# Earlier operands at a seam, additions by twos, a second attention output tile and a second load queue in a fused block kernel

## The chip, the cores and the metric

The kernel runs on one core of one Trainium2 chip. The metric is the device time of one execution in microseconds (us); of several executions the median is given. Five engines work side by side, each on its own list of instructions: PE (matrix multiplies), DVE and ACT (element by element), POOL and SP (here almost only the issuing of transfers). An instruction whose input or output tile is not yet free blocks everything behind it in the list of its engine.

## The reference, cut to what matters

```
h = rmsnorm(x, norm_g)                              # 2048 tokens x 1024
q, k, v, z_att, gb, gc, u, z_conv, g_att, g_conv = split(h @ w_in)   # 1024 x 6144
att    = chunked_rel_attention(q, k, v, rel_bias)   # 8 heads of 64, a band of 9 chunks of 64 tokens
y_att  = (att * silu(z_att)) @ w_att_out            # 512 x 1024
y_conv = (gb * causal_conv3(gc * u) * silu(z_conv)) @ w_conv_out
m = sigmoid(g_att) * y_att + sigmoid(g_conv) * y_conv
x = x + m @ w_out                                   # 1024 x 1024
out = rmsnorm(x, final_norm_g)
```

Everything is float32.

## The kernel before

**Split numbers.** Every float32 operand is held as two tiles: a rounded high part, cast by ACT (`nc.scalar.copy`), and the rest, subtracted by DVE (`nc.vector.tensor_sub`). `split_into` does that for weights (L130, L131), `split_pair` for tokens (L136, L137). A product is then three matmuls per 128 rows of depth: high by high (L143), high by low (L144), low by high (L145), in `passes`.

**Products of blocks.** The big projection takes the tokens in two halves of 1024, each as two chunks of 512 (`CH`), and the 6144 columns as 24 pairs of two 128-column tiles (`NPAIR`). For one pair and one half, tokens, weights and results form 2 by 2 blocks, and the four result blocks come from seven block products, i = 1 to 7, in place of eight, with sums and differences of blocks as operands. One block product is four depth tiles by three passes, twelve matmuls of 128 x 512. The token operands `t{i}{j}` (product i, depth tile j) are made once for each half by `operand_steps`: for i = 6, 4 and 5 one DVE addition or subtraction (L363, L365, L369), and then the split on ACT and DVE. The weight operands `wc` of a pair are made by `operand(p, i)`, three block products ahead, and kept in DRAM for the second half (L408, L390, both on SP).

**The plain stage.** The first three pairs (`PLAIN`) of the first half are multiplied plainly, before the tokens are normalized, as twelve items q = 0 to 11 of 24 matmuls each (result `ps_p`, copied by ACT to `plain`, L727). This stage is in a `tc.manual_schedule`: there PE, DVE and ACT do the work in the order of the code. `between(q)` puts `steps` of `operand_steps` behind items 6 to 10, one operand i each; behind item 10 (`c and n == 0` of the last pair) two calls of `operand` make the weights of the products 1 and 2 of the first block pair. Everywhere else a scheduler sets each engine's order, and `seq` is the order of the block products.

**Attention.** From the second half on, attention runs interleaved with the block products: scores into `ps_s` (L199) with the bias and the minimum on DVE (L205), exponential and scaling on ACT (`pr`, L209, L211), transposes into `ps_t` (L219), the split of these into `pt` (ACT L224, DVE L225), and the product with the values into `po` (L234). `po` is added up into the output tile `o` of a pair of heads (DVE, L239, L240); when a chunk of 512 tokens of the pair is done, `o` is multiplied by `z`, split into `zs` and `o`, and both are stored by POOL as `mid` (L248). The tile `o` exists once. POOL also loads the attention's operands, among them `q` (L165) and `zs` (L187).

**Output projections.** `half_c` multiplies the `mid` tiles by `wy`, `half_d` the sum by `w_out`. The first sixteen `mid` tiles (those of the convolution) are loaded by SP (`load_mid`, L566) near the end of the block products.

Of the kernel before, what the change touches and what calls it, by code (L numbers as in the profile page):

```python
# [8 lines left out]
F32 = mybir.dt.float32  # L9
# [8 lines left out]
P = 128  # L18
# [5 lines left out]
CH = 512  # L24
NC = SEQ // CH
HEADS = 8
DH = 64
# [6 lines left out]
PLAIN = 3  # L34
# [8 lines left out]
def block_kernel(ctx, tc, xb, xt, wp_in, wy, wo, bias, ng, fg, cw, cb, out):  # L43
    nc = tc.nc
    pool = lambda name, bufs=1, **k: ctx.enter_context(tc.tile_pool(name=name, bufs=bufs, **k))

    const = pool("const")
    small = pool("small", 3)
    dram = pool("dram", 1, space=DRAM)

    ident = const.tile([P, P], F32, name="ident")
# [22 lines left out]
    def inverse_rms(v, n):  # L74

        y = small.tile([P, n], F32, name="ry", tag="ry")
        a = small.tile([P, n], F32, name="ra", tag="ra")
        q = small.tile([P, n], F32, name="rq", tag="rq")
        nc.vector.tensor_scalar(y.bitcast(I32), v.bitcast(I32), -0.5, 0x5F3759DF, op0=ALU.mult, op1=ALU.add)
        nc.vector.tensor_mul(a, y, v)  # L80
        nc.vector.scalar_tensor_tensor(a, a, THIRD, y, op0=ALU.mult, op1=ALU.mult)
        nc.vector.scalar_tensor_tensor(q, a, -10.0 / 3.0 * THIRD, a, op0=ALU.add, op1=ALU.mult)
        nc.vector.scalar_tensor_tensor(y, q, 5.0 * THIRD * THIRD, y, op0=ALU.add, op1=ALU.mult)
        nc.vector.tensor_mul(a, y, v)
        nc.vector.scalar_tensor_tensor(a, a, -0.5 / D_MODEL, y, op0=ALU.mult, op1=ALU.mult)
        nc.vector.scalar_tensor_tensor(y, a, 1.5, y, op0=ALU.add, op1=ALU.mult)
        return y

    def rms_of(acc, n):

        v = small.tile([P, n], F32, name="rv", tag="rv")
        nc.vector.scalar_tensor_tensor(v, acc[:, 0:2 * n:2], D_MODEL * EPS, acc[:, 1:2 * n:2], op0=ALU.add, op1=ALU.add)
        return inverse_rms(v, n)

# [23 lines left out]
    def defer(n, fn):  # L118
        later.append([n, fn])
# [20 lines left out]
    def passes(ps, w, rhs, cs=slice(0, CH), first=True, last=True, onto=False):  # L140

        for k, (rh, rl) in enumerate(rhs):
            nc.tensor.matmul(ps, lhsT=w[:, 0, k, :], rhs=rh[:, cs], start=(first and not onto and k == 0), stop=False, skip_group_check=onto)  # L143
            nc.tensor.matmul(ps, lhsT=w[:, 0, k, :], rhs=rl[:, cs], start=False, stop=False, skip_group_check=onto)  # L144
            nc.tensor.matmul(ps, lhsT=w[:, 1, k, :], rhs=rh[:, cs], start=False, stop=(last and k == len(rhs) - 1), skip_group_check=onto)  # L145


    def attention(ab):
# [35 lines left out]
        def load_z(c, h):  # L184
            if h % 2 == 0:
                zs = at([P, CH], "zs", F32)
                dma(zs, z_d[h // 2][c])  # L187
                pair[c, h // 2] = (zs, at([P, CH], "o", F32))

        def att_s(c, h, g):  # L190
            q, kk, bs = heads[c, h]
# [154 lines left out]
    def split_t(half, i, j, src):  # L346
        ops[half, i, j] = split_pair(f"t{i}{j}", src)
# [9 lines left out]
    def operand_steps(half):  # L357

        b11, b12, b21, b22 = (blocks[half, c, k] for k in range(2) for c in range(2))
        for i in ORDER:  # L360
            for j in range(4):
                if i == 6:
                    nc.vector.tensor_add(b11[:, j, :], b11[:, j, :], b12[:, j, :])  # L363
                elif i == 4:
                    nc.vector.tensor_sub(b21[:, j, :], b21[:, j, :], b11[:, j, :])  # L365
                src = {1: b11, 2: b21, 6: b11, 7: b12, 4: b21, 3: b22}.get(i)
                if i == 5:
                    t1 = e("t1")
                    nc.vector.tensor_sub(t1, b22[:, j, :], b11[:, j, :])  # L369
                split_t(half, i, j, t1 if i == 5 else src[:, j, :])  # L370
            yield i


# [73 lines left out]
    def ev_v(pr):  # L447
        def ev(g, c, src):
            t = copied_out(src)

            def turn():
                ps = bank("vt") if g < 2 else dbank("vt")
                for b in range(4):
                    nc.tensor.transpose(out=ps[:, b * P:(b + 1) * P], in_=t[:, b * P:(b + 1) * P], identity=ident)
                defer(0, lambda: split(ps))

            def split(ps):
                for b in range(2):
                    st = e("vst").rearrange("p (n d) -> p n d", d=P)
                    s = ps[:, b * 256:(b + 1) * 256].rearrange("p (n d) -> p n d", d=DH)  # L460
                    nc.scalar.copy(st[:, :, :DH].bitcast(F32R), s)
                    nc.vector.tensor_sub(st[:, :, DH:].bitcast(F32R), s, st[:, :, :DH])
                    v4 = st.rearrange("p (b h) d -> p b h d", h=2)
                    for h in range(2):
                        n = g % 2 * 4 + 2 * b
                        defer(1, lambda h=h, v4=v4, n=n: store(v_d[2 * pr + h][g // 2][:, n:n + 2, :], v4[:, :, h, :]))

            defer(1, turn)
        return ev
# [90 lines left out]
        nc.sync.dma_start(r4, src)  # L560
        return r4

    def load_mid(i, b, c):
        t = [slot("mid") for s in range(2)]
        for s in range(2):
            nc.sync.dma_start(t[s].bitcast(F32), mid_d[i][b][s][c])  # L566
        return t

    def gate(i, d, c, make):
# [92 lines left out]
    nw = 0  # L662
# [19 lines left out]
        return ss  # L682

    def rsqrt_of(ss):
        v = small.tile([P, 4], F32, name="rv", tag="rv")
        nc.vector.tensor_scalar_add(v, ss[:, 0:8:2], D_MODEL * EPS)
        return inverse_rms(v, 4)

    def between(q):

        if q == 4 or q == 5:
            for k in range(8):
                normalize(tt_[q - 4][k], k, rb[q - 4])
        elif q == 6:
            for j in range(4):
                third(0, j)
        if q > 5 and len(built) < 5:
            built.append(next(steps))

    engines = {mybir.EngineType.PE, mybir.EngineType.DVE, mybir.EngineType.Activation}  # L700
# [1 line left out]
    with tc.manual_schedule(engines=engines):  # L702
        for k in range(2):
            weights0(0, 0, k)
            for j in range(4):
                raw_split(0, 4 * k + j, tt_[0][4 * k + j])
        for k in range(2):
            weights0(0, 1, k)
        for k in range(8):
            square(0, k)  # L710
        for q, (p, n, c) in enumerate(plain):
            if q == 2:
                ss[0] = sums_of(0)
            elif q == 4:
                rb[0] = inverse(ry[0], e)
                store(rb_d[0], rb[0])
            ps = dbank("ps_p")
            for k in range(2):
                if k and q == 4:
                    ss[1] = sums_of(1)  # L720
                    ry[1] = rsqrt_of(ss[1])
                elif k and q == 5:
                    rb[1] = inverse(ry[1], e)
                    store(rb_d[1], rb[1])
                passes(ps, wops0[p, n, k], [raw_ops[c, 4 * k + j] for j in range(4)], slice(0, CH), k == 0, k == 1)
            t = e("plain")
            nc.scalar.copy(t, ps)  # L727
            store(plain_d[q], t)
            between(q)
            if q == 0:  # L730
                for j in range(8):
                    raw_split(1, j, tt_[1][j])
            elif q == 1:
                for k in range(4):
                    square(1, k)
            elif q == 2:
                ry[0] = rsqrt_of(ss[0])
                for k in range(4, 8):
                    square(1, k)
            if c and p + 1 < PLAIN:  # L740
                for k in range(2):
                    weights0(p + 1, n, k)
            elif c and n == 0:
                for _ in range(2):
                    operand(*seq[nw])
                    nw += 1
    x1 = None
    nbias = 0
    att = None
# [7 lines left out]
    for s, (p, i) in enumerate(seq):  # L757
# [17 lines left out]
        if n == 5 and i == 1:  # L775
            for c in range(2):
                for k in range(2):
                    load_x(1, c, k)
            x1 = norm_steps(1)
        ev = evs[p % NPAIR]  # L780
        g0, g1 = 2 * half, 2 * half + 1
        onto = half == 0 and i in (6, 5, 4, 3)
# [82 lines left out]
        if n == 2 * NPAIR - 1 and i == 5:  # L865
            made = make_c(0, ITEMS_C[0], e)
            rbs = [fslot("rbs") for c in range(2)]
            for c in range(2):
                nc.sync.dma_start(rbs[c], rb_d[c])
            mids = {c: [load_mid(1, b, c) for b in range(4)] for c in (0, 1)}  # L870
    while later:
        tick()
    for _ in ab:
# [34 lines left out]
    pair_slot = lambda: op.tile([P, 2, CH], F32R, tag="op", name="wo")  # L908
    wide_slot = lambda: wtile("wo").rearrange("p s k c -> p s (k c)")

    def half_c(hf, mids, made):

        cs = (2 * hf, 2 * hf + 1)
        c0, c1 = cs
# [25 lines left out]
        for n_, (i, d) in enumerate(ITEMS_C):  # L940
            raw, gl = made
            if n_ + 1 < len(ITEMS_C):
                made = make_c(hf, ITEMS_C[n_ + 1])
            w = wtile("wy")
            split_into(w, raw)
            if d < PLAIN and not hf:
                for c in cs:
                    nc.vector.tensor_mul(gl[c], gl[c], rbs[c])
# [199 lines left out]
        elif n == 3:  # L1148
            nxt["made"] = make_c(1, ITEMS_C[0])

    half_d(0, half_c(0, mids, made), next_half)
    half_d(1, half_c(1, nxt["mids"], nxt["made"]), lambda n: None)


# [49 lines left out]
```

## Time and profile before

| | |
|---|---|
| median of 3 runs | 1495.09 us (1494.68 to 1496.42) |
| the profiled execution, device time | 1495.93 us |
| its span in the trace | 1494.2 us |
| TensorE clock granted, mean | 0.997 of full |
| PE busy | 1474.8 us (99%) |
| DVE, ACT, POOL busy | 1074.0, 743.7, 163.8 us |
| plain stage, block products, output projections | to about 78, about 78 to 1157, from about 1157 us |

Times of places in the program count from the start of the span. A line such as L143 is line 143 of the kernel before. A row of the timeline gives start, duration, engine, line, operation, output<-input, shape and count, and in brackets how long the engine had been idle and what released it. A row of the waits gives who waits, at which line, for whom, the total in us, how often, and the longest. SPq stands for issues by SP.

### The profile page before, as it was taken

Reading aid. Unit: us, or ns where it says so; the run is one execution under the profiler, and the core shown is the slowest. Engines: PE = TensorE matmul, PEld = TensorE weight load, DVE = VectorE, ACT = ScalarE, POOL = GpSimd, SP = SyncE. Lnnn points to the kernel's source line nnn. Section 1 sums busy time; section 2 is a strip of 40 time slices with the busy share of each in tenths; the row PEclk is TensorE's granted clock in tenths of the full one; section 3 lists DMA queues with packets and bytes.
Section 4 is the critical chain, followed back from the end, with each engine's and each line's share of the span. In section 5 each row is a group of like instructions: output and inputs, shape, how many; then the busy total and the mean of one; then the engine's idle time right before and its main releaser. Section 6 shows DMA issues by size and latency. Waiting matters only on the chain. (4 is left out here: it accounts for less than half of the span.)

```text
span 1494.2 us, 21053 instructions
## 1 busy us (share of the span) xinstructions
PE 1474.8 (99%) x6976; PEld 1225.2 (82%) x6976; DVE 1074.0 (72%) x2100; ACT 743.7 (50%) x1407; POOL 163.8 (11%) x310
## 2 busy tenths in 40 slices
PE   9999999999999999999999999999999999999997
PEld 6878888888888788888888888788888788888886
DVE  7877567686568684766777778787766588767787
ACT  7454444444346333555666666566665333423153
POOL 0000000000000002323222233322220000010000
PEclk9999999999999999999999999999999999999999
DMA  6389999989989976999999787787889845877443
GB/s 235 104 308 334 336 323 331 372 315 330 323 299 329 342 288 234 322 359 346 308 293 286 243 269 256 237 261 257 271 278 324 296 152 173 304 261 232 155 162 113
DMA packets 169325, 409.33 MB, mean 274 GB/s; under 512 B 21120, under 2 KB 41600, under 8 KB 169216
## 3 DMA queue, kind: packets, MB, share of 16 engines
q1 hardware_dynamic: 139312, 320.67, 62.1%
q0 software_dynamic: 22272, 73.42, 15.4%
q10 hardware_dynamic: 7632, 13.90, 2.5%
q8 instruction: 55, 0.90, 0.2%
q14 instruction: 54, 0.44, 0.1%
HBM read 252.19 MB, written 155.71 MB: 273 GB/s over the span
## 5 line engine op out<-in xcount | busy, mean ns | idle before, releaser
L209 ACT ACTIVATE pr<-ps_s,nmax 128x640 f32<-128x640 f32 (+4 forms) x128 | 93.4, 730 | 94.6 <-DVE nmax L205 93.9
L165 POOL DMA_DIRECT2D q<-q x128 | 66.8, 526 | 662.9 <-DVE wc L131 572.8
L211 ACT ACTIVATE pr<-pr,rs 128x640 f32<-128x640 f32 (+4 forms) x128 | 97.8, 764 | 36.0 <-DVE rs L210 35.6
L205 DVE CUSTOM_DVE_ANT_0 ps_s<-ps_s,bs 128x640 f32<-128x640 f32 (+4 forms) x128 | 95.2, 744 | 23.3 <-PE ps_s L199 22.1
L131 DVE TENSOR_TENSOR wc<-wraw,wc 128x512 fp32r<-128x512 f32 x120 | 81.7, 685 | 30.9 <-ACT wc L130 30.6
L143 PE MATMUL ps_d<-mid,wy 128*128 128x512 f32 x256 | 100.1, 391 | 1.4 <-ACT wy L130 0.8
L144 PE MATMUL ps_d<-mid,wy 128*128 128x512 f32 x256 | 99.7, 390 | 0.2 <-DMA mid<-mid 0.2
L199 PE MATMUL ps_s<-kk,q 128*128 128x320 f32 (+1 forms) x448 | 98.3, 334 | 1.5 <-ACT pr L209 0.9
L145 PE MATMUL ps_d<-mid,wy 128*128 128x512 f32 x256 | 99.6, 390 | 0.0
L130 ACT CAST wc<-wraw 128x512 fp32r<-128x512 f32 x120 | 73.7, 621 | 46.0 <-PE ps_c L145 20.0
L225 DVE TENSOR_TENSOR pt<-ps_t,pt 128x640 fp32r<-128x640 f32 (+4 forms) x128 | 94.0, 735 | 3.4 <-ACT pt L224 2.5
L224 ACT CAST pt<-ps_t 128x640 fp32r<-128x640 f32 (+4 forms) x128 | 79.9, 624 | 21.2 <-PE ps_t L219 20.0
L219 PE MATMUL ps_t<-ident,pr 128*128 128x128 f32 x560 | 82.3, 273 | 1.3 <-DVE pt L225 1.2
L234 PE MATMUL po<-pt,vv 128*128 128x512 f32 x336 | 75.2, 355 | 0.3 <-DVE pt L225 0.3
L219 PEld LDWEIGHTS ps_t<-ident,pr 128*128 128x128 f32 x560 | 65.6, 140 | 11.4 <-DVE pt L225 1.6
L234 PEld LDWEIGHTS po<-pt,vv 128*128 128x128 f32 x336 | 62.4, 188 | 14.2 <-DVE pt L225 1.2
L199 PEld LDWEIGHTS ps_s<-kk,q 128*128 128x128 f32 x448 | 67.3, 189 | 6.6 <-ACT pr L209 5.8
L1001 PE MATMUL ps_w<-wo,lefth 128*128 128x512 f32 (+1 forms) x240 | 71.9, 382 | 0.0
L903 ACT ACTIVATE wo<-wor 128x512 fp32r<-128x512 f32 x56 | 34.5, 630 | 60.6 <-DMA wor<-wo 42.2
L143 PEld LDWEIGHTS ps_d<-mid,wy 128*128 128x128 f32 x256 | 48.1, 188 | 12.8 <-ACT wy L130 1.2
L145 PEld LDWEIGHTS ps_d<-mid,wy 128*128 128x128 f32 x256 | 48.1, 188 | 10.5 <-DVE wy L131 0.5
L144 PEld LDWEIGHTS ps_d<-mid,wy 128*128 128x128 f32 x256 | 48.1, 188 | 10.3 <-DMA mid<-mid 0.5
(557 smaller groups left out, 4089.5 us busy)
## 6 DMA issues: line engine op xcount, KB each, us to landing
wc<-wc SPq DMA_DIRECT2D x294, 512.0 KB, 5.4
wraw<-wp_in SPq DMA_DIRECT2D x54, 512.0 KB, 5.7
q<-q POOLq DMA_DIRECT2D x128, 128.0 KB, 4.9
mid<-mid SPq DMA_DIRECT2D x64, 256.0 KB, 5.5
wor<-wo SPq DMA_DIRECT2D x56, 256.0 KB, 5.0
gl<-gate SPq DMA_DIRECT2D x52, 256.0 KB, 2.9
bs<-bias POOLq DMA_DIRECT2D x32, 320.0 KB, 7.6
v<-vst SPq DMA_DIRECT2D x64, 128.0 KB, 4.4
```

The source lines that it names most:

```text
L131: nc.vector.tensor_sub(w[:, 1], src, w[:, 0].bitcast(F32))
L143: nc.tensor.matmul(ps, lhsT=w[:, 0, k, :], rhs=rh[:, cs], start=(first and not onto and k == 0), stop=False, skip_group_check=onto)
L144: nc.tensor.matmul(ps, lhsT=w[:, 0, k, :], rhs=rl[:, cs], start=False, stop=False, skip_group_check=onto)
L145: nc.tensor.matmul(ps, lhsT=w[:, 1, k, :], rhs=rh[:, cs], start=False, stop=(last and k == len(rhs) - 1), skip_group_check=onto)
L199: nc.tensor.matmul(ps[:, i, :m], lhsT=q[s][:, g * P:(g + 1) * P], rhs=kk[:, k1 - n + i * m:k1 - n + (i + 1) * m], start=(s == 0), stop=(s ...
L205: nc.vector.tensor_tensor_reduce(out=view, in0=view, in1=bv, scale=-0.125, scalar=3.0e38, op0=ALU.add, op1=ALU.min, accum_out=nmax)
L209: nc.scalar.activation(out, view, AF.Exp, bias=nmax, scale=-1.0, accum_out=rs)
L211: nc.scalar.activation(pr[:, :n], pr[:, :n], AF.Identity, scale=rs)
L219: nc.tensor.transpose(out=ps[:, j * P:(j + 1) * P], in_=pr[:, j * P:(j + 1) * P], identity=ident)
L224: nc.scalar.copy(hi[:, js, qs], src)
L225: nc.vector.tensor_sub(lo[:, js, qs], src, hi[:, js, qs].bitcast(F32))
L234: nc.tensor.matmul(ps[:, :, a * P:b * P], lhsT=vv[:, g0 + j, :], rhs=pt[:, j, :, a * P:b * P], start=(i == 0), stop=(i == len(js) - 1))
```

## The change

1. **End of the plain stage.** One weight operand is made before the copy of item 10 in place of two behind it, the second one follows that copy; the plain stage takes four token operands (1, 2, 6, 7) and not five; and the first half makes its token operands in the order 1, 2, 6, 7, 5, 4, 3, in which its products use them.
2. **Tokens two at a time.** In `operand_steps` two additions (or subtractions) stand ahead of their two splits, in place of addition, split, addition, split. This holds for both halves.
3. **V stores.** V is split for each head apart, and 32 stores of 4 x 128 per partition take the place of 64 of 2 x 128.
4. **Output tile.** `o` gets two buffers; two of the small vector pools go from three buffers to two for the space.
5. **First `mid` tiles.** POOL loads them in place of SP.
6. **First weights of the output projection.** `wy0` is allocated and split in the code of the last block product, and handed to `half_c`.

```diff
     small = pool("small", 3)
+    two = pool("two", 2)
...
-                pair[c, h // 2] = (zs, at([P, CH], "o", F32))
+                pair[c, h // 2] = (zs, at([P, CH], "o", F32, 2))
...
-        for i in ORDER:
-            for j in range(4):
-                if i == 6:
-                    nc.vector.tensor_add(b11[:, j, :], b11[:, j, :], b12[:, j, :])
-                elif i == 4:
-                    nc.vector.tensor_sub(b21[:, j, :], b21[:, j, :], b11[:, j, :])
-                src = {1: b11, 2: b21, 6: b11, 7: b12, 4: b21, 3: b22}.get(i)
-                if i == 5:
-                    t1 = e("t1")
-                    nc.vector.tensor_sub(t1, b22[:, j, :], b11[:, j, :])
-                split_t(half, i, j, t1 if i == 5 else src[:, j, :])
+        for i in ORDER if half else (1, 2, 6, 7, 5, 4, 3):
+            src = {1: b11, 2: b21, 6: b11, 7: b12, 4: b21, 3: b22}.get(i)
+            at = [None if i == 5 else src[:, j, :] for j in range(4)]
+            for js in ((0, 1), (2, 3)):
+                for j in js:
+                    if i == 6:
+                        nc.vector.tensor_add(at[j], at[j], b12[:, j, :])
+                    elif i == 4:
+                        nc.vector.tensor_sub(at[j], at[j], b11[:, j, :])
+                    elif i == 5:
+                        at[j] = e("t1")
+                        nc.vector.tensor_sub(at[j], b22[:, j, :], b11[:, j, :])
+                for j in js:
+                    split_t(half, i, j, at[j])
             yield i
...
-                for b in range(2):
+                p4 = ps.rearrange("p (n h d) -> p n h d", h=2, d=DH)
+                for h in range(2):
...
-                    for h in range(2):
-                        n = g % 2 * 4 + 2 * b
-                        defer(1, lambda h=h, v4=v4, n=n: store(v_d[2 * pr + h][g // 2][:, n:n + 2, :], v4[:, :, h, :]))
+                    n = g % 2 * 4
+                    defer(1, lambda h=h, st=st: store(v_d[2 * pr + h][g // 2][:, n:n + 4, :], st))
...
-        if q > 5 and len(built) < 5:
+        if q > 5 and len(built) < 4:
             built.append(next(steps))
...
+            if q == 4 * PLAIN - 2:
+                operand(*seq[nw])
+                nw += 1
             t = e("plain")
             nc.scalar.copy(t, ps)
...
-                for _ in range(2):
-                    operand(*seq[nw])
-                    nw += 1
+                operand(*seq[nw])
+                nw += 1
...
+        if s == len(seq) - 1:
+            wy0 = wtile("wy")
+            split_into(wy0, made[0])
...
-            mids = {c: [load_mid(1, b, c) for b in range(4)] for c in (0, 1)}
+            mids = {c: [load_mid(1, b, c, nc.gpsimd.dma_start) for b in range(4)] for c in (0, 1)}
...
-    half_d(0, half_c(0, mids, made), next_half)
+    half_d(0, half_c(0, mids, made, wy0), next_half)
```

How the order of instructions moves is shown at three places; line numbers of after stand one to ten higher.

On ACT, at the end of the plain stage, before the change (`t73h` is the last split of operand 7, `t40h` to `t43h` are those of operand 4; `plain` is the result of item 10 and then of 11; `wc` are the weights of products 1 and 2):

```order
L136 CAST t73h_1161<-xs_558 128x512
L727 COPY plain_1190<-ps_p_1165 128x512
L136 CAST t40h_1194<-xs_553 128x512
L136 CAST t41h_1199<-xs_553 128x512
L136 CAST t42h_1204<-xs_553 128x512
L136 CAST t43h_1209<-xs_553 128x512
L130 CAST wc_1213<-wraw_572 128x512
L130 CAST wc_1216<-wraw_572 128x512
L727 COPY plain_1244<-ps_p_1219 128x512
```

And after the change:

```order
L137 CAST t73h_1164<-xs_561 128x512
L131 CAST wc_1193<-wraw_575 128x512
L733 COPY plain_1196<-ps_p_1168 128x512
L131 CAST wc_1199<-wraw_575 128x512
L131 CAST wc_1231<-s2_1233 128x512
L131 CAST wc_1239<-wraw_577 128x512
L733 COPY plain_1227<-ps_p_1202 128x512
L131 CAST wc_1262<-s1_1232 128x512
```

The first `wc` stands directly behind `t73h`; the splits of operand 4 have gone from this stretch, and the weights of products 6 and 7 (`s2` and the next `wraw`) stand in it.

On DVE, in one of the attention's steps late in the second half, before the change (`c` and `u` are results of block products, `ot` and `o` the attention's output, `pt` the split of the transposed weights, ISA the bias and minimum of the scores):

```order
L798 TENSOR_TENSOR c_9641<-u,ps_d 128x512
L239 TENSOR_TENSOR ot<-po,ot 64x256
L240 TENSOR_TENSOR o<-po,ot 64x256
L225 TENSOR_TENSOR pt<-ps_t,pt 128x5x128
L205 ISA ps_s,nmax<-ps_s,bs 128x2x320
L205 ISA nmax 128x1
L820 TENSOR_TENSOR u<-u,ps_d 128x512
L210 RECIPROCAL rs<-rs 128x1
```

And after the change:

```order
L806 TENSOR_TENSOR c_9612<-u,ps_d 128x512
L240 TENSOR_TENSOR ot<-po,ot 64x256
L241 TENSOR_TENSOR o<-po,ot 64x256
L206 ISA ps_s,nmax<-ps_s,bs 128x2x320
L206 ISA nmax 128x1
L226 TENSOR_TENSOR pt<-ps_t,pt 128x5x128
L211 RECIPROCAL rs<-rs 128x1
L828 TENSOR_TENSOR u<-u,ps_d 128x512
```

`o` stands at the same place in the list, the scores' reduction has moved ahead of `pt`, and `rs` ahead of `u`; with two buffers the `o` of this step is another tile than the one still being stored.

On SP near the end of the block products, before the change (`mid1` are the stored tiles of the convolution, the last four of sixteen; `mid0` are the attention's):

```order
L566 DMA mid_11863<-mid1_2_0_1_268 128x512
L566 DMA mid_11864<-mid1_2_1_1_272 128x512
L566 DMA mid_11867<-mid1_3_0_1_276 128x512
L566 DMA mid_11868<-mid1_3_1_1_280 128x512
L566 DMA mid_11910<-mid0_0_0_0_219 128x512
```

After the change the same loads stand on POOL, behind the load of the last `z` and ahead of the stores of the last attention output:

```order
L569 DMA mid_11834<-mid1_2_0_1_271 128x512
L569 DMA mid_11835<-mid1_2_1_1_275 128x512
L569 DMA mid_11838<-mid1_3_0_1_279 128x512
L569 DMA mid_11839<-mid1_3_1_1_283 128x512
L249 DMA mid0_3_0_3_249<-zs_11492 128x512
L249 DMA mid0_3_1_3_253<-o_11494 128x512
```

On SP the loads of `mid0` then follow the last `wc` directly. The rows of ACT around the first cast of `wy` (behind the last `zs`) read alike in both orders: part 6 moves no row there.

More of the change, by code (lines that the diff above doesn't have):

```diff
@@ L76, in inverse_rms @@
         y = small.tile([P, n], F32, name="ry", tag="ry")
-        a = small.tile([P, n], F32, name="ra", tag="ra")
+        a = two.tile([P, n], F32, name="ra", tag="ra")
         q = small.tile([P, n], F32, name="rq", tag="rq")
@@ L89, in rms_of @@
     def rms_of(acc, n):
-        v = small.tile([P, n], F32, name="rv", tag="rv")
+        v = two.tile([P, n], F32, name="rv", tag="rv")
         nc.vector.scalar_tensor_tensor(v, acc[:, 0:2 * n:2], D_MODEL * EPS, acc[:, 1:2 * n:2], op0=ALU.add, op1=ALU.add)
@@ L457, in split @@
             def split(ps):
-                for b in range(2):
+                p4 = ps.rearrange("p (n h d) -> p n h d", h=2, d=DH)
+                for h in range(2):
                     st = e("vst").rearrange("p (n d) -> p n d", d=P)
-                    s = ps[:, b * 256:(b + 1) * 256].rearrange("p (n d) -> p n d", d=DH)
+                    s = p4[:, :, h, :]
                     nc.scalar.copy(st[:, :, :DH].bitcast(F32R), s)
                     nc.vector.tensor_sub(st[:, :, DH:].bitcast(F32R), s, st[:, :, :DH])
-                    v4 = st.rearrange("p (b h) d -> p b h d", h=2)
-                    for h in range(2):
-                        n = g % 2 * 4 + 2 * b
-                        defer(1, lambda h=h, v4=v4, n=n: store(v_d[2 * pr + h][g // 2][:, n:n + 2, :], v4[:, :, h, :]))
+                    n = g % 2 * 4
+                    defer(1, lambda h=h, st=st: store(v_d[2 * pr + h][g // 2][:, n:n + 4, :], st))
             defer(1, turn)
@@ L561, in raw_w, with load_mid @@
         return r4
-    def load_mid(i, b, c):
+    def load_mid(i, b, c, dma=nc.sync.dma_start):
         t = [slot("mid") for s in range(2)]
         for s in range(2):
-            nc.sync.dma_start(t[s].bitcast(F32), mid_d[i][b][s][c])
+            dma(t[s].bitcast(F32), mid_d[i][b][s][c])
         return t
@@ L684, in rsqrt_of @@
     def rsqrt_of(ss):
-        v = small.tile([P, 4], F32, name="rv", tag="rv")
+        v = two.tile([P, 4], F32, name="rv", tag="rv")
         nc.vector.tensor_scalar_add(v, ss[:, 0:8:2], D_MODEL * EPS)
@@ L909, in block_kernel, with half_c @@
     wide_slot = lambda: wtile("wo").rearrange("p s k c -> p s (k c)")
-    def half_c(hf, mids, made):
+    def half_c(hf, mids, made, ready=None):
         cs = (2 * hf, 2 * hf + 1)
@@ L943, in half_c @@
                 made = make_c(hf, ITEMS_C[n_ + 1])
-            w = wtile("wy")
-            split_into(w, raw)
+            w, ready = ready, None
+            if w is None:
+                w = wtile("wy")
+                split_into(w, raw)
             if d < PLAIN and not hf:
```

## The prediction

> **What bounds the kernel now.** I read the page's shares first, then what PE waited for, then the timeline around each wait.
>
> ```profile
> PE 1474.8 (99%) x6976; PEld 1225.2 (82%) x6976; DVE 1074.0 (72%) x2100; ACT 743.7 (50%) x1407; POOL 163.8 (11%) x310
> DMA  6389999989989976999999787787889845877443
> ```
>
> PE is busy for all but 1494.2 − 1474.8 = 19.4 us. The change removes no matmul, so it can win only PE's gaps and what follows from them: a matmul issued at half pace counts as busy. The second line is the share of the transfer engines in tenths, per fortieth of the span: often 9, so a queue may be a limit that PE's busy time hides.
>
> The waits of PE (at which line, for whom, total us, how often, longest):
>
> ```profile
> PE ps_c L143 <- ACT wc L130: 2.6, 1, 2.6
> PE ps_t L219 <- DVE pt L225: 1.2, 2, 1.0
> PE ps_d L143 <- DMA wc<-wc: 1.1, 1, 1.1
> PE ps_s L199 <- ACT pr L209: 0.9, 1, 0.9
> PE ps_d L143 <- ACT wy L130: 0.8, 1, 0.8
> PE po L234 <- DVE pt L225: 0.3, 1, 0.3
> PE ps_c L145 <- DVE wc L131: 0.3, 1, 0.3
> ```
>
> Each is a single place, not a steady shortage. The windows (from:to and length; busy us and count of PE, PEld, DVE, ACT, POOL; granted clock; DMA share; GB/s) show what else the two largest places cost:
>
> ```profile
> 75.00:112.00 37.00, 34.42 (x145) 27.95 (x144) 27.81 (x45) 19.96 (x36) 0.00 (x0) 0.95 0.87 310
> 112.00:150.00 38.00, 38.00 (x170) 31.45 (x169) 27.07 (x46) 15.99 (x27) 0.00 (x0) 1.00 0.93 333
> 934.00:972.00 38.00, 36.04 (x186) 30.40 (x185) 27.11 (x59) 22.72 (x41) 11.31 (x21) 0.96 0.74 237
> ```
>
> The granted clock is 0.95 and 0.96 there, and 1.00 in the undisturbed middle row. So a gap there costs its own length and a stretch at lower clock behind it.
>
> **Part 1, the end of the plain stage.** The timeline (start, duration, instruction; in brackets the idle time before it and its releaser):
>
> ```profile
> 71.98 0.62 ACT L136 CAST t73h<-xs 128x512 fp32r<-128x512 f32 x1
> 72.89 0.68 DVE L137 TENSOR_TENSOR t73l<-xs,t73h 128x512 fp32r<-128x512 f32 x1
> 78.17 0.62 ACT L136 CAST t42h<-xs 128x512 fp32r<-128x512 f32 x1 [1.36 <-DVE xs L365]
> 78.37 0.39 PE L145 MATMUL ps_p<-rawh,w 128*128 128x512 f32 x1
> 80.15 0.62 ACT L136 CAST t43h<-xs 128x512 fp32r<-128x512 f32 x1 [1.36 <-DVE xs L365]
> 80.67 1.14 ACT L130 CAST wc<-wraw 128x512 fp32r<-128x512 f32 x2
> 81.34 0.50 PE L143 MATMUL ps_c<-t10h,wc 128*128 128x512 f32 x1 [2.58 <-ACT wc L130]
> 85.36 0.39 PE L145 MATMUL ps_c<-t12h,wc 128*128 128x512 f32 x1
> 91.83 0.69 DVE L137 TENSOR_TENSOR t53l<-t,t53h 128x512 fp32r<-128x512 f32 x1
> 93.97 0.39 PE L143 MATMUL ps_c<-t50h,wc 128*128 128x512 f32 x1
> 96.69 0.39 PE L143 MATMUL ps_c<-t10h,wc 128*128 128x512 f32 x1
> ```
>
> ACT is held by the splits of operand 4, one per 1.98 us (78.17 to 80.15), each waiting 1.36 us for its DVE subtraction; the first cast of `wc` stands behind them at 80.67, and PE, out of plain work at 78.37, waits. At full pace PE starts a matmul every 2.72/12 = 0.2267 us (93.97 to 96.69 is one block product). Without the wait, the first block matmul starts at 78.37 + 0.23 = 78.60 and the eleventh at 80.87. It started at 85.36: ten matmuls took 4.02 us in place of 2.27. Loss: 85.36 − 80.87 = **4.49 us**.
>
> In the new order `wc` stands right behind `t73h`: its cast can end at 72.60 + 0.62 = 73.2, its DVE part, behind `t73l` (ends 73.57), at about 74.3. It is needed at 78.60, so 4.3 us of margin cover it. What is late next? The plain copies wait behind one or two casts of 0.62 us, for a bank needed 5.4 us later (24 matmuls). Operand 5, used fifth, was ready at 91.83 + 0.69 = 92.52 and is now needed at 78.60 + 4 × 2.72 = 89.5. Operand 4's four rounds no longer stand before it: 4 × 1.98 = 7.9 earlier gives 84.6, and with the extra weight splits and copies placed ahead of it at their durations I get 87.4. Operand 4 then has until 97.7, and is ready by about 91.3. Cover of 2 us or more everywhere; if it is gone, the cost is the lateness and, past about 2 us, the slow matmuls again. I take the whole 4.49, with 0.5 less to nothing more as bounds.
>
> How a gap leads to slow matmuls: a gap of 2.58 us was followed by ten at 0.40 us. The Trainium skill, "TensorE: Matmul & The Clock Gate", section "HAM oscillation — how this bites in real kernels", holds that gaps of PE are harmless for the clock up to about 3.4 us. This trace differs: 2.58 us, and 1.01 + 0.95 us below, were enough. By the page only the idle time itself could be won at both places (rival 2).
>
> **Part 4, the second output tile.** The wait of DVE in the whole span, and the timeline at its longest:
>
> ```profile
> DVE o L240 <- DMA mid<-o: 6.9, 5, 2.8
> ```
>
> ```profile
> 943.10 0.57 POOL L248 DMA_DIRECT2D mid<-o  x1
> 945.28 0.69 ACT L224 CAST pt<-ps_t 128x640 fp32r<-128x640 f32 x1 [0.18 <-PE ps_t L219]
> 948.19 0.39 PE L145 MATMUL ps_d<-t63h,wc 128*128 128x512 f32 x1
> 948.38 0.42 DVE L240 TENSOR_TENSOR o<-po,ot 64x256 f32<-64x256 f32 x1 [2.83 <-DMA mid<-o]
> 948.73 0.81 DVE L225 TENSOR_TENSOR pt<-ps_t,pt 128x640 fp32r<-128x640 f32 x1
> 949.59 0.77 PE L219 MATMUL ps_t<-ident,pr 128*128 128x128 f32 x5 [1.01 <-DVE pt L225]
> 956.33 1.31 PE L234 MATMUL po<-pt,vv 128*128 128x512 f32 x6
> 957.49 0.71 PE L219 MATMUL ps_t<-ident,pr 128*128 128x128 f32 x5
> 961.37 0.71 PE L219 MATMUL ps_t<-ident,pr 128*128 128x128 f32 x5
> ```
>
> The sum into `o` waits until POOL's store of the previous `o`, issued at 943.10, has read it; `pt` stands behind it on DVE, and PE's transposes need the bank that `pt` reads. PE stood 1.01 us, then 0.95 for `pr` (the row above), and ran slowly. Transposes, scores and a block product take 961.37 − 957.49 = 3.88 us at full pace. Due at 948.19 + 0.23 = 948.42, the same work would end, and `po` start, at 952.30; it started at 956.33. Loss: **4.03 us**. With two tiles `o` starts at 948.38 − 2.83 = 945.55, and the reduction and `pt` behind it (about 0.8 each) end near 947.6, 0.8 us before PE needs them. This is the thinner margin: if another row of DVE slips in, part of it returns. The two other waits of PE on `pt` (1.2 − 1.01 = 0.2, and 0.3) stand behind smaller waits of this kind: **0.50 us** more. Bounds for the sum: 2.5 (the idle alone) to 4.53. The pools cut to two buffers hold values of a dozen short DVE rows; nothing in the waits named them: 0.
>
> **Part 2, additions by twos.** The 1.36 us that ACT idles before each split of a round become shared by two tokens, which moves DVE work earlier by a fraction of a microsecond in each half. PE only sees it where it waited:
>
> ```profile
> 484.33 0.68 DVE L131 TENSOR_TENSOR wc<-wraw,wc 128x512 fp32r<-128x512 f32 x1
> 490.11 0.45 SPq L390 DMA_DIRECT2D wc<-wc  x1
> 498.17 0.47 PE L143 MATMUL ps_d<-t20h,wc 128*128 128x512 f32 x1 [1.14 <-DMA wc<-wc]
> ```
>
> SP's stores and loads wait in line for the `wc` made at 484.33, and the load issued at 490.11 lands 8.06 us later, with the transfer engines nearly full; PE waits 1.1 us. In the new order that `wc` stands some 1.6 us earlier on DVE. If SP follows wholly, the 1.1 us are gone; if the landing is set by the queues alone, nothing is. Bounds 0 to 1.2, taken **0.6**. The 0.3 us on `wc` (L131) lies in the same stretch: taken 0, bounds ±0.3.
>
> **Part 3, V stores.** Half the issues, the same bytes, and no row of PE's waits names V: 0. **Part 6, `wy0`.** ACT keeps its order (`zs`, then `wy`), so the 0.8 us stay: 0, bounds 0 to 0.75 won.
>
> **Part 5, the first `mid` tiles.**
>
> ```profile
> L165 POOL DMA_DIRECT2D q<-q x128 | 66.8, 526 | 662.9 <-DVE wc L131 572.8
> 1136.59 12.72 SPq L566 DMA_DIRECT2D mid<-mid  x16
> 1157.27 0.54 POOL L248 DMA_DIRECT2D mid<-zs  x1 [27.54 <-ACT zs L245]
> 1157.55 0.50 PE L143 MATMUL ps_d<-mid,wy 128*128 128x512 f32 x1 [0.75 <-ACT wy L130]
> ```
>
> POOL has nothing for 27.54 us before 1157.27, so the sixteen loads have that time; at 526 ns each (the issues of `q`) they take 8.4 us. Their tiles come free as before, by about 1137. They would be issued by about 1146 and, even at the 8.06 us of the loaded queue above, land by 1154; PE needs the first at 1157.55. Hidden: 0, with 3.5 us of cover. Queued behind them are only the two `mid` stores, used a whole half later. SP loses 12.72 us of issuing and can only be earlier.
>
> **Sum.** 4.49 + 4.03 + 0.50 + 0.60 = 9.62 us. The profiled execution took 1495.93 us, so 1486.3; it lies 0.84 above the median of 1495.09, so against the median **1485.5 us**.
>
> **The rivals.**
>
> 1. *One of the two big places stays, or a wait of that size takes its place.* For it: 0.8 us of margin at 947.6; 1.44 us of work more on DVE there brings the loss back. Against: every other place has 2 us. The sum without 4.03 gives 1489.5, without 4.49 gives 1490.0.
> 2. *The slow matmuls do not come from the gaps.* Then only idle time goes: 2.58 + 1.96 + 0.50 + 0.60 = 5.64, so 1489.5. Against it: the clock is below 1.00 in just these two windows, and the pace recovers behind both; the 1.1 us gap at 497 shows no slow stretch, so a threshold below 1.96 is what the rows suggest. It is the page's rule as a mechanism.
> 3. *Transfers are the bound, and time won at 78 us is given back at the next load.* For it: share 0.93 at 112 to 150. Against: PE has its 38.00 us of 38.00 there, with no wait on a load until 497. If PE ran into the queue, the 4.49 and 0.6 would be lost as later gaps, and with slow matmuls behind them the rest: about 1494.5, no change.
> 4. *POOL issues the sixteen loads late* (the other side). POOL is free from 1157.27 − 27.54 = 1129.7. To land by 1157.55, at 8.06 us a load, the last must be issued by 1149.5: 1.2 us each is where it begins to cost. At 3 us each the last is issued at 1178 and landed at 1186, 28 us late, of which the first chunk's products fill some 8: about 1505. Against: `q` took 526 ns with DVE busy 72% of the time. The Trainium skill, "SBUF — State Buffer", section "🔬 SBUF: two separate sides", tells of a POOL-issued transfer of 620 ns that takes 3100 ns beside a DVE copy; the row of `q` does not show it here.
>
> **The chances.** Forecast 0.74; rival 1 0.14, rival 2 0.03, rival 3 0.05, rival 4 0.04. About 0.2% (3.0 us) is what a measurement of this kernel can tell from no change. Faster: 0.74 + 0.14 + 0.03 = 0.91; same 0.05; slower 0.04. The forecast's own range is 1483.6 (the rest of the wait at 497, `wy` and the 0.3 on `wc` won as well, and 0.2 of spread between executions: 9.62 + 0.6 + 0.75 + 0.3 + 0.2 = 11.5) to 1487.5 (2 us of the terms missed). To hold 8 in 10 it reaches over rivals 1 and 2: 1483.6 to 1491.0.
>
> **What would show it.** Right: PE's waits without `wc` (L130) and without `pt` of 1 us; PE's first block matmul 0.23 us after the last plain one; clock 1.00 in windows like 75 to 112 and 934 to 972; no DVE wait of `o` on `mid`; POOL's sixteen loads near 0.5 us each, ended before 1150. Wrong: a new PE gap of 2 us or more with a lower clock behind it, first of all at operand 5 (about 89 us) or at `pt`; PE waiting for `mid`; or a gap at 497 grown by what was won before it.

## The result, and the profile after

The changed kernel takes 1486.26 us (median of 4 runs, 1485.22 to 1488.41), the kernel before 1494.88 us (4 runs, 1493.53 to 1496.42). The medians lie 8.6 us apart; the ratio of the runs side by side is 0.9938, with a 95% interval of 0.9923 to 0.9954. Forecast were 1485.5 us and a range of 1483.6 to 1491.0. The profiled execution took 1487.22 us, its span 1485.4 us. Line numbers of after stand one to ten higher than before.

The page's shares, and then PE's waits (who, at which line, for whom, total us, times, longest):

```profile
PE 1471.6 (99%) x6976; PEld 1222.4 (82%) x6976; DVE 1074.0 (72%) x2100; ACT 743.5 (50%) x1407; POOL 172.6 (12%) x326
```

```profile
PE ps_p L144 <- ACT rawh L354: 2.1, 1, 2.1
...
PE ps_d L144 <- ACT wy L131: 0.7, 1, 0.7
PE ps_c L144 <- ACT u L811: 0.7, 2, 0.5
...
PE ps_d L144 <- ACT gl L959: 0.2, 1, 0.2
PE ps_t L220 <- DVE pt L226: 0.2, 1, 0.2
```

PE's gaps fell from 19.4 to 1485.4 − 1471.6 = 13.8 us, by 5.6; PE's busy time fell by 3.2 us with the same matmuls, above all because the stretches at half pace are gone. The rows for `wc` and `pr` have vanished. The first row stands at 8 us, ahead of everything that the change touches (0.9 us before); the first product starts at 8.39 us for 8.42 before, so it costs nothing. A new row has come: `ps_c` waits for ACT's copy `u`. The two windows of the big waits, and the timeline at the end of the plain stage:

```profile
75.00:112.00 37.00, 37.00 (x165) 30.66 (x164) 25.87 (x42) 19.94 (x38) 0.00 (x0) 1.00 0.96 356
...
934.00:972.00 38.00, 38.00 (x205) 32.24 (x205) 30.00 (x65) 25.32 (x45) 12.37 (x23) 1.00 0.79 257
```

```profile
72.63 0.68 DVE L132 TENSOR_TENSOR wc<-wraw,wc 128x512 fp32r<-128x512 f32 x1
...
78.34 0.39 PE L146 MATMUL ps_p<-rawh,w 128*128 128x512 f32 x1
78.57 0.39 PE L144 MATMUL ps_c<-t10h,wc 128*128 128x512 f32 x1
```

The weights are ready at 73.31, the first block matmul follows the last plain one after 0.23 us, and the clock is 1.00 in both windows. At the attention step of 948 us (now near 940) `o` stands without a wait, and `pt` ends at 942.63, 0.96 us before PE's transposes need its bank:

```profile
940.74 0.42 DVE L241 TENSOR_TENSOR o<-po,ot 64x256 f32<-64x256 f32 x1
941.82 0.81 DVE L226 TENSOR_TENSOR pt<-ps_t,pt 128x640 fp32r<-128x640 f32 x1
942.90 0.39 PE L144 MATMUL ps_d<-t63h,wc 128*128 128x512 f32 x1
...
943.59 0.71 PE L220 MATMUL ps_t<-ident,pr 128*128 128x128 f32 x5
```

Where the time went is read best by setting each matmul against the same one of before. The lead of the changed kernel is the start of a matmul before minus its start after, here as the median over stretches of 10 us of these two profiles. Its changes make a ledger:

| place, us | change of the lead | predicted |
|---|---|---|
| 78, end of the plain stage | +4.50 | +4.49 |
| 240 to 325, ACT `u` | −1.89 | 0 |
| 443 and 460, DVE `wc` and next | +0.9 | 0 |
| 497, transfer of `wc` | +1.34 | +0.60 |
| 550 | +0.5 | 0 |
| 696, attention | +0.61 | +0.50 |
| 948, `o` | +3.96 | +4.03 |
| 600 to 1150, all along in attention | −1.6 | 0 |
| 1182 and 1203, `mid`, `gl` | +1.3 | 0 |
| 1250 to PE's last matmul, last projection | −1.3 | 0 |
| behind PE's last matmul | +0.4 | 0 |

The two large terms came out within 0.1 us. The rows that were not forecast, or not in that size, nearly cancel (−4.8 and, with the whole of 497, +4.4), and they are what the experiments are about. A short wait of PE takes more from the lead than its idle time: at 242 us 0.21 us idle took 0.5. The trace counts idle time from the end of the matmul before, 0.39 us after its start, while at full pace the next one starts after 0.23 us. So the waits on `u`, 0.7 us idle at four places, took 1.89.

### The profile page after: what moved, and what is told of

It is laid out like the page before. It is cut to its first block, busy times and chain, and to the rows that moved or that the text cites. A ratio compares the mean times of both kernels' runs of the same rounds, so it can differ in the third digit from the quotient of the medians.

```text
span 1485.4 us, 21018 instructions
## 1 busy us (share of the span) xinstructions
PE 1471.6 (99%) x6976; PEld 1222.4 (82%) x6976; DVE 1074.0 (72%) x2100; ACT 743.5 (50%) x1407; POOL 172.6 (12%) x326
## 5 line engine op out<-in xcount | busy, mean ns | idle before, releaser
L146 PEld LDWEIGHTS ps_d<-mid,wy 128*128 128x128 f32 x256 | 48.0, 188 | 10.5 <-DVE wy L132 0.5
```

## The experiments

Each ratio is to the kernel before, run on the same chip beside it.

**Part 1 alone: `seam`.** The three hunks of part 1 on the kernel before, with additions and splits by turns as before:

```diff
-        for i in ORDER:
+        for i in ORDER if half else (1, 2, 6, 7, 5, 4, 3):
...
-        if q > 5 and len(built) < 5:
+        if q > 5 and len(built) < 4:
...
+            if q == 4 * PLAIN - 2:
+                operand(*seq[nw])
+                nw += 1
```

> Part 1 alone on the kernel before (1494.9 us). Theory: PE gains 4.5 us at the end of the plain stage (first block matmul at about 78.6), and gives back about 1.9 us between 240 and 325 us, because the raw weights' loads come forward by less than PE does and ACT's copy u loses its 0.3 to 0.8 us of slack before the fifth product; PE waits for ACT u appear there. 2.6 us are left, with 0 to 2 us more from the places at 443 and 497: 1490.3 to 1492.3 us. Rival: the 1.9 us are given back because of the other parts (additions by twos, V stores); then there is no wait on u here and the time is 1490.4 or less, with the lead of 4.5 us kept up to 440 us.

1491.56 us, ratio 0.9979 (0.9968 to 0.9989). The lead is 4.35 us after the plain stage, and falls by 1.57 us at one place, with these waits of PE:

```profile
PE ps_d L143 <- DMA wc<-wc: 1.4, 1, 1.4
PE ps_c L143 <- ACT u L805: 1.3, 1, 1.3
```

So the wait on `u` needs neither part 2 nor part 3, and the wait at 497 is not removed by part 1. But the wait on `u` came at 205 us, once, not at 240 to 320. The lead also grew by 1.4 us between 1175 and 1205 us, without part 5.

**Part 4 alone: `twotiles`.** Second `o`, and the two small pools.

```diff
+    two = pool("two", 2)
...
-                pair[c, h // 2] = (zs, at([P, CH], "o", F32))
+                pair[c, h // 2] = (zs, at([P, CH], "o", F32, 2))
```

> Part 4 alone (second output tile, two pools cut to two buffers) on the kernel before. Theory: nothing moves up to 660 us, the small waits on pt give 0.5 us, the place at 948 gives 4.0 us, the clock of that window is 1.00: 1490.4 us. Rival: most of the gain at 948 came from the new order of the scores' reduction and pt, or from elsewhere; it can be told here only if the wait of o on the store is gone and PE still stands still, with a time over 1492.

1491.98 us, ratio 0.9975 (0.9965 to 0.9985). The windows show that only the second place is cured:

```profile
75.00:112.00 37.00, 34.34 (x145) 27.81 (x145) 27.79 (x45) 19.84 (x36) 0.00 (x0) 0.95 0.83 300
934.00:972.00 38.00, 38.00 (x208) 32.69 (x207) 29.83 (x65) 26.17 (x47) 12.05 (x23) 1.00 0.80 255
```

The lead rises by 4.0 us at 948 and by 0.6 at 696, and shrinks by a slow drift all through attention and the last projection, as in the changed kernel. The new order of the scores' reduction and `pt` on DVE comes with the second tile here too; it puts `pt` 0.7 us later, so it is not what won the time. `seam` has no such drift: its lead stays between 2.99 and 3.17 us from 560 to 1150.

**Without part 2: `no_twos`,** and **without part 5: `mid_sp`.**

```diff
-            for js in ((0, 1), (2, 3)):
+            for js in ((0,), (1,), (2,), (3,)):
```

> The changed kernel (1486.3 us) with additions and splits by turns again, one token tile at a time. Theory: part 2 gave the gains at 443 us (0.6) and 497 us (1.3): both waits come back, 1488.2 us; the waits on u between 240 and 325 us stay. Rival: these two gains come from PE's other timing towards the transfers (part 1), so the time stays at 1486.3. Second rival: part 2 causes the waits on u, so they are gone and the time is about 1486.3 - 1.9 + 1.9 with the lead at 440 us at 4.5.

```diff
-            mids = {c: [load_mid(1, b, c, nc.gpsimd.dma_start) for b in range(4)] for c in (0, 1)}
+            mids = {c: [load_mid(1, b, c) for b in range(4)] for c in (0, 1)}
```

> The changed kernel with the first sixteen mid tiles loaded by SP again. Theory: the 1.3 us won between 1157 and 1205 us (waits on mid at 1182 and on gl at 1203) came from taking these loads off SP's queue: both come back, 1487.6 us. Rival: they came with the general shift, and the time stays at 1486.3.

`no_twos`: 1486.74 us, 0.9945 (0.9931 to 0.9959). `mid_sp`: 1485.72 us, 0.9939 (0.9926 to 0.9951). Against 0.9938 for the whole change, both parts are worth nothing that shows. Both first theories fell: `no_twos` had no wait at 443 or 497, and none on `u`; `mid_sp` gained 0.9 us of lead between 1175 and 1205, where the changed kernel gained 1.3.

**Without part 3: `no_v`,** and **the changed kernel once more: `again`.** In `no_v` the V split and its 64 stores are those of before.

```diff
-                    defer(1, lambda h=h, st=st: store(v_d[2 * pr + h][g // 2][:, n:n + 4, :], st))
+                    for h in range(2):
+                        n = g % 2 * 4 + 2 * b
+                        defer(1, lambda h=h, v4=v4, n=n: store(v_d[2 * pr + h][g // 2][:, n:n + 2, :], v4[:, :, h, :]))
```

> The changed kernel with the old V stores (64 of 2 x 128 per partition). Theory: the waits at 443 us (DVE wc, with its slow matmuls 0.6 us) and 497 us (transfer of wc, 1.3 us) are gone because 32 stores less stand on SP; both come back here: 1486.3 + 1.9 = 1488.2 us. Rival: they are gone because of part 1 with part 2, or by chance of an execution; then they stay away and the time is 1486.3 us.

> The changed kernel unchanged, a second profile. Theory: the small waits on ACT u between 200 and 325 us (1.9 us in all in the first profile) differ from one execution to the next, since the loads' landing does: other places and another sum, 0 to 2.5 us; the slower matmuls of attention and ps_w (391 ns) come again, as they follow from the program. Rival: the waits follow from the program too, and stand again at 242, 262, 300 and 320 us with 1.9 us.

`no_v`: 1488.4 us, 0.9957 (0.9943 to 0.9971). `again`: 1486.4 us, 0.994 (0.9926 to 0.9953). The waits of `no_v`:

```profile
PE ps_c L144 <- ACT u L812: 2.4, 3, 1.4
...
PE ps_d L144 <- DMA wc<-wc: 0.4, 1, 0.4
PE ps_c L146 <- DVE wc L132: 0.3, 1, 0.3
```

Both places of before are back (443 us: 0.3 idle, 497 us: 0.4), so it is the old V stores that bring them. `no_v` is 2.0 us slower than `again`, by the medians of runs side by side. The wait on `u` is settled by a window over the stretch, of the changed kernel's first profile, of `again` and of `no_v`:

```profile
200.00:330.00 130.00, 129.31 (x571) 105.75 (x570) 94.45 (x184) 57.29 (x109) 0.00 (x0) 1.00 0.91 331
```

```profile
200.00:330.00 130.00, 130.00 (x579) 107.64 (x578) 97.58 (x189) 59.43 (x111) 0.00 (x0) 1.00 0.93 341
```

```profile
200.00:330.00 130.00, 128.25 (x568) 105.32 (x567) 94.85 (x187) 58.98 (x114) 0.00 (x0) 1.00 0.91 335
```

The same program has PE busy for all of the 130 us in one execution and lacks 0.69 us in another. The wait belongs to the execution. Nor did it cost anything in the end: `again` came to 1160 us with a lead of 10.5 us and lost 0.7 there up to 1205, where the first profile gained 1.3, and the two executions took 1487.15 and 1487.22 us.

**Part 3 alone: `v_only`.**

> Part 3 alone (32 V stores of 4 x 128 per partition) on the kernel before. Theory: these stores hold up SP and the V splits hold up DVE where the first half ends; without them the waits at 443 us (DVE wc) and 497 us (transfer of wc) are gone, 0.6 + 1.3 us: a ratio of about 0.9987 to the kernel before; the waits at 78 and 948 us stay. Rival: the two waits go only together with part 1; then they stay here and the ratio is 1.000.

1492.11 us, ratio 0.9973 (0.9962 to 0.9984), which means 4.0 us, more than the theory's 1.9. The profiled execution was the slowest of the seven, with 1496.12 us (span 1494.4). It shows

```profile
PE ps_t L219 <- DVE pt L225: 2.9, 2, 2.3
PE ps_c L143 <- ACT wc L130: 2.7, 1, 2.7
...
PE ps_d L143 <- DMA wc<-wc: 0.2, 1, 0.2
```

The wait at 443 is gone and that at 497 down from 1.1 to 0.2 us; the lead rises there by 0.8 and 0.95 us, close to the theory's 1.9 in all. (The 0.5 at 550 came as well, but also in `seam` and `twotiles`, with the old stores; it is not part 3's.) What else of the 4.0 is part 3's stays open: this profile is not a typical one (its wait of `pt` at 948 was 2.3 us, for 1.0 before).

How part 3 removes the wait at 443 shows on DVE, in the kernel before and then in `v_only`:

```profile
440.71 0.42 DVE L462 TENSOR_TENSOR vst<-vt,vst 128x256 fp32r<-128x256 f32 x1 [1.66 <-ACT vst L461]
441.05 0.68 DVE L399 TENSOR_TENSOR s<-wraw 128x512 f32<-128x512 f32 x1
...
442.98 1.28 DVE L131 TENSOR_TENSOR wc<-wraw,wc 128x512 fp32r<-128x512 f32 x2
```

```profile
439.36 0.68 DVE L399 TENSOR_TENSOR s<-wraw 128x512 f32<-128x512 f32 x1
...
441.11 0.43 DVE L463 TENSOR_TENSOR vst<-vt,vst 128x256 fp32r<-128x256 f32 x1 [1.07 <-ACT vst L462]
...
442.65 1.29 DVE L131 TENSOR_TENSOR wc<-wraw,wc 128x512 fp32r<-128x512 f32 x2
```

The V split has as many subtractions as before. But the scheduler now puts the addition `s`, work for the weights, ahead of a subtraction that waits for its cast (`vst`), and no longer behind it, so `wc` is done 0.3 us earlier while PE is 0.4 us later. The order is the old one in `seam`, `twotiles`, `pools_only` and `no_v`, and the new one in the changed kernel and the other kernels with part 3 and the same order of products. Why the scheduler orders it so is not shown.

**More slack for `u`: `late5`.** Product 1 of the next pair goes ahead of product 5.

```diff
-        seq += [(p, 6), (p, 7), (p, 5), (nxt, 1), (nxt, 2), (p, 4), (p, 3)]
+        seq += [(p, 6), (p, 7), (nxt, 1), (p, 5), (nxt, 2), (p, 4), (p, 3)]
```

> The changed kernel with product 1 of the next pair ahead of product 5 in the first half, so that ACT's copy u has 2.7 us more before product 5 needs it. Theory: no wait on u is left, the lead of 4.5 us lasts to 440 us: 0 to 2 us faster than the changed kernel, 1484.4 to 1486.3 us, and the spread of its runs is smaller. Rival: the raw weights, due 2.7 us earlier, become the wait instead (PE on wc): same or slower than 1486.3 us.

1502.04 us, ratio 1.0041 (1.0025 to 1.0056): slower than before. `u` is no longer waited for, but

```profile
PE ps_c L144 <- DVE v L817: 7.3, 8, 1.6
```

Product 4 accumulates into the bank that the addition `v` reads, and with product 5 later `v` has one product to finish in, not two. Neither expectation named this wait.

**Addresses alone: `pools_only` and `aligned`.** In `pools_only` only the two pools are cut, and every engine's order is that of before; the token, weight and small working tiles on the left side of SBUF lie 64 bytes lower. `aligned` is the changed kernel with `ry` and `rq` in the pool of two buffers too, again in the order of the changed kernel: these tiles lie 128 bytes lower than before. Its edit:

```diff
-        y = small.tile([P, n], F32, name="ry", tag="ry")
+        y = two.tile([P, n], F32, name="ry", tag="ry")
...
-        q = small.tile([P, n], F32, name="rq", tag="rq")
+        q = two.tile([P, n], F32, name="rq", tag="rq")
```

> The kernel before with the two small vector pools cut to two buffers and nothing else; the order of every engine is as before, only tile addresses move by some bytes. Question: in the kernels with part 4 the matmuls of attention and of the last projection took about 0.4% longer (391 ns for 389 in ps_w, 396 for 393 in po), some 2 us in all, which the prediction had not. Theory: the moved addresses do it; then ps_w takes 391 ns here and the time is 1.5 to 2 us above before (about 0.1%). Rival: the second output tile does it (the attention's tiles, POOL's transfers); then ps_w takes 389 ns and the time is that of before.

> The changed kernel with two more small values (ry, rq) in the pool of two buffers: the order of every engine is that of the changed kernel, and the tiles behind the small pools lie 128 bytes lower than in the kernel before, not 64. Theory: the slower matmuls of attention and of the last projection come from the 64 bytes; with 128 ps_w takes 389 ns and po 393 ns again, and the time is 1.5 to 2 us below the changed kernel: about 1484.6 us. Rival: any move of these tiles does it, or the values with two buffers; then ps_w stays at 391 ns and the time at 1486.3 us.

`pools_only`: 1497.84 us, ratio 1.0012 (1.0001 to 1.0022). `aligned`: 1486.82 us, 0.9948 (0.9934 to 0.9962). The groups of matmuls by shape (busy us, mean ns), of before, of `pools_only` and of `aligned`:

```profile
L1001 PE MATMUL ps_w<-wo,lefth 128*128 128x512 f32 x224 | 69.0, 389 | 0.0
L234 PE MATMUL po<-pt,vv 128*128 128x512 f32 x224 | 62.0, 393 | 0.3 <-DVE pt L225 0.3
```

```profile
L1002 PE MATMUL ps_w<-wo,lefth 128*128 128x512 f32 x224 | 69.4, 391 | 0.0
L235 PE MATMUL po<-pt,vv 128*128 128x512 f32 x224 | 62.9, 396 | 0.7 <-DVE pt L226 0.7
```

```profile
L1011 PE MATMUL ps_w<-wo,lefth 128*128 128x512 f32 x224 | 70.0, 394 | 0.0
L235 PE MATMUL po<-pt,vv 128*128 128x512 f32 x224 | 62.1, 393 | 0.0
```

64 bytes alone make both groups 2 to 3 ns slower. This holds in every profile: 389 and 393 ns in the three without the move, 391 and 395 to 396 in the eight with 64 bytes, 394 and 393 in the two with 128. The larger part of the drift in attention comes from the block products beside it: between 570 and 1140 us their matmuls with the high part of the tokens take 231 ns from start to start on the mean (`pools_only`), for 229 before. Moved by 128, `po` is back at 393 ns and the drift in attention is gone, but `ps_w` takes 394 ns, and the last projection loses what attention won. So the theory held for one stage and not for the other; the placement does it, no rule for a good one is found, and the total is that of the changed kernel, not the expected 1484.6.

`pools_only` shows two more things. It has the old end of the plain stage and one `o`:

```profile
PE ps_t L220 <- DVE pt L226: 1.5, 1, 1.5
...
PE ps_c L144 <- ACT u L804: 1.0, 3, 0.5
...
PE ps_s L200 <- ACT pr L210: 0.9, 1, 0.9
```

```profile
934.00:972.00 38.00, 35.50 (x189) 29.65 (x188) 28.55 (x62) 23.06 (x42) 11.31 (x21) 1.00 0.78 256
```

PE waits for `u` here without part 1 (and for 0.5 us in `v_only`). And near 948 PE stood for 1.47 and then 0.95 us, longer than before, but no slow stretch followed: the matmuls came every 0.23 us, the clock is 1.00, and the place cost some 3.0 us of lead in place of 4.0.

**Three parts: `three_parts`.** Parts 1, 3 and 4 on the kernel before, with the pools of `aligned`.

> The kernel before with parts 1, 3 and 4 alone, and the small pools as in the kernel aligned. Theory: parts 2, 5 and 6 are worth nothing, so this is as fast as aligned, about 1484.6 us, with no wait at 443, 497 and 948. Rival: the small gains at 1182 and 1203 us need part 5, or the place at 497 part 2: then 1 to 2 us slower than aligned.

1486.64 us, ratio 0.9953 (0.994 to 0.9965), the same as `aligned` and 2 us above the expected 1484.6, with no wait at 443, 497 and 948. The rival is not seen. No variant is clearly faster than the changed kernel.

## Why the prediction was right, and which steps were not

- **End of the plain stage, 4.49 us:** shown. 4.50 in the changed kernel, 4.5 in `seam`, with nothing late behind it; operand 5's first product starts at 89.45, as forecast (89.5).
- **Second output tile, 4.03 us:** shown by `twotiles`, 4.0, against a profile of before with a slow stretch behind the gap; some 1.5 us of it are that stretch, which `pools_only` had not. The margin of `pt` was 0.96 us for the predicted 0.8. Of the 0.50 us for the smaller waits, that on `po` at 696 went; that of 0.2 on `pt` near 660 stayed.
- **Rival 2** (slow matmuls not from the gaps) is out: with each gap the half pace behind it went, at each place separately. But a gap does not always bring it. The first one, 2.58 to 2.84 us, did so in all four kernels that have it (clock 0.95). The Trainium skill ("TensorE: Matmul & The Clock Gate", section "HAM oscillation — how this bites in real kernels") names gaps of more than about 3.4 us; here these shorter ones were enough. The pair near 948 did so in the kernel before (1.01 + 0.95 us, clock 0.96), in `seam` (1.25 + 0.95, 0.96) and in `v_only` (2.32 + 0.81, 0.91), and did not in `pools_only` (1.47 + 0.95, 1.00). Single gaps up to 1.60 us (in `late5` at 277 us, clock 1.00 from 270 to 285) were never followed by one. So the prediction's threshold "below 1.96" is no fixed one. Its price for rival 2, the idle time alone, also leaves out the 0.3 us that every gap takes besides.
- **V stores, costed at nothing:** the failed step. "No row of PE's waits names V" was read as no effect. But the V work shares SP's and DVE's lists with the `wc` on which PE did wait at 443 and 497; these two places are 0.9 + 1.3 us of the ledger, go with part 3 (`v_only`) and come back without it (`no_v`). With the old stores and the same order of products, PE stands 0.3 us at 443 in every profile, and 0.4 to 1.4 us at 497; with the new ones not at all at 443, and at most 0.25 us at 497. At 443 it is DVE's order that does it. At 497, whether SP's fewer issues or the transfers themselves do it is not separated.
- **Additions by twos, 0.6 us at 497:** wrong attribution. `seam` (without part 2) and `no_v` (with it) keep the wait; `no_twos` (with part 3 and without part 2) has it not. Part 2 is worth nothing measurable.
- **"Cover of 2 us or more everywhere":** wrong for ACT's `u` before product 5, which I did not price. Before, `u` ended at 246.48 for a matmul at 246.78. The chain behind it starts with the raw weights' landing, which in the first profile of the changed kernel came forward by 3.90 us while PE came forward by 4.52:

```profile
238.43 0.69 DVE L399 TENSOR_TENSOR s<-wraw 128x512 f32<-128x512 f32 x1 [4.03 <-DMA wraw<-wp_in]
...
245.91 0.57 ACT L803 COPY u<-ps_c 128x512 f32<-128x512 f32 x1
```

```profile
234.53 0.69 DVE L403 TENSOR_TENSOR s<-wraw 128x512 f32<-128x512 f32 x1 [4.30 <-DMA wraw<-wp_in]
...
242.02 0.56 ACT L811 COPY u<-ps_c 128x512 f32<-128x512 f32 x1
242.63 0.50 PE L144 MATMUL ps_c<-t50h,wc 128*128 128x512 f32 x1 [0.21 <-ACT u L811]
```

  This looks like rival 3 in small: 1.9 us of 4.5 returned in one execution, none in `again`. But that PE's lead brings the wait is not shown: `again`, `no_twos` and `aligned` have the same lead and no such wait, `pools_only` and `v_only` have the wait and no part 1. The row of that addition `s` moved by itself: in `again` it started 6.25 us earlier than before (232.18) with PE 4.7 us ahead, in `pools_only` 1.6 us later (240.04) with PE 0.7 us behind. A slack of 0.3 us is too little for that.
- **Pools cut, costed at nothing:** wrong by some 1.8 us (`pools_only`, 1.0012; 0.1 to 3.3 us by its interval) or 2.9 us by the ledger's two drifts, not by waits but by the addresses that moved.
- **POOL's `mid` loads, 0:** right; rival 4 did not come. They took 0.55 us each beside a busy DVE (with additions and reductions; no copy of DVE's stood beside them, so what one would do is not tested), the last was issued at 1137.68 (forecast: by 1146), and PE had its first product at 1149.16:

```profile
1122.58 3.77 POOL L569 DMA_DIRECT2D mid<-mid  x7 [0.62 <-PE ps_d L146]
...
1137.68 0.55 POOL L569 DMA_DIRECT2D mid<-mid  x1 [0.59 <-DMA mid<-mid]
```

- **`wy0`, 0:** right; the wait is 0.7 us for 0.8.
- The 1.3 us at 1182 and 1203 also came in `seam` and `twotiles`; which of before's waits there belong to its one profile is not settled.

The two large terms were right in place and in size. That the sum of 9.6 us came so close to the measured 8.6 is luck besides: unpriced gains and losses nearly cancelled.

## What to carry to other kernels

A gap of the matrix engine can cost more than its idle time, by a slow stretch behind it: measure to the first matmul at full pace again, take such gaps away whole, and do not count on the slow stretch in every execution. A part that no wait names can still be what delays the instruction that is named: follow the list of that engine back before costing it at nothing. Before reading a difference of 1 us from two profiles, take the same program's profile twice.

## What the runs showed of the hardware

Moving tiles by 64 bytes, with every engine's order unchanged, made most matmuls in attention and in the last projection 2 to 4 ns slower (389 to 391 ns, 393 to 396 in `pools_only`) and the kernel 0.12% slower (0.01 to 0.22%). The `po` matmuls of 256 columns became faster (281 to 278 ns). In the block products of the first half the same move changed no pace: the lead of `twotiles` stays between −0.08 and −0.03 us from 100 to 430 us. The operands of the block products had moved, those of `po` had not, so it is not simply the address of what the matmul reads; the cause is open.

Two waits of PE close together (1.47 and 0.95 us, with five transposes between them) were followed by matmuls at full pace in one execution, and shorter ones (1.01 and 0.95 us) by eight matmuls at 0.43 us in place of 0.23 in another.
